# A hybrid decoder layer: TensorE's order in the second part written out as a list, with larger banks and weight pieces

## The chip, the cores and the metric

The kernel runs on one core of a Trainium2 chip. [...] Each engine works through its own instructions in order, and semaphores tie the engines together. The metric is the device time of one launch in microseconds (us).

## The reference

One decoder layer on 256 tokens of width 1024, with two attention branches side by side and an output that must hold in float32. The listing is shortened from the reference's description and its functions.

```python
D_MODEL = 1024; SEQ = 256; MLA_HEADS = MOBA_HEADS = 8      # one sequence, one layer
def one_layer(x, c, positions, p):                          # "a" is MLA, "b" is MoBA
    mod = silu(c) @ W_ada + b_ada;  shift, scale, gate = split(mod)
    h = rms_norm(x, g_pre) * (1 + scale) + shift
    q_lat, kv_lat, k_rope, gate_a, q_b, k_b, v_b, gate_b, merge = split_cols(h @ W_in, IN_SIZES)
    # branch a: queries and keys of 64 + 32 (rope) per head, from latents of rank 256 and 128
    q = rms_norm(q_lat, g_q) @ W_uq;  k_nope, v = split(rms_norm(kv_lat, g_kv) @ W_ukv)
    o_a = causal_dense_attention(concat(q_nope, rope(q_pe)), concat(k_nope, rope(k_rope)), v, 96 ** -0.5)
    # branch b: 64 per head; 256 tokens are one block, so each token sees its own block, causally
    o_b = causal attention of (rope(q_b), rope(k_b), v_b), scale 64 ** -0.5
    y_a = (o_a * silu(gate_a)) @ W_o_a;  y_b = (o_b * silu(gate_b)) @ W_o_b
    y = (sigmoid(merge_a) * y_a + sigmoid(merge_b) * y_b) @ W_out
    return x + gate * rms_norm(y, g_post)
```

## The kernel before

**Accuracy sets the work.** Each float32 operand is split into a rounded part and a remainder, `w1 = round(w)` and `w2 = w - w1`, and each product is three matmuls, `w1·h1 + w1·h2 + w2·h1`. A weight arrives by DMA in a raw tile of 2048 columns, and is split in units of 1024 columns: ACT writes `w1` (L264, `w<-raw`), DVE writes `w2` (L264, `w<-raw,w`). Five units and five raw tiles are alive at a time (`RING`, `RAW`), so a split waits until TensorE has finished the unit five before it. Before, each unit is split in two halves of 512 columns.

**Two parts.** The first part (to 61 us) computes the modulation, the normalised input `h` and the projections of branch b; its order stays as it is. The second part holds all else: 24 units `F` (gates and merge gates; L417 to L419, 24 matmuls of 128x256 each, into the bank "acc"), the latents of branch a (`lat_mm`, L501 to L503), and for each of 16 heads scores, a softmax (DVE and ACT, L660 to L669), three transposes of the probabilities (`p_tr`, L676) and the product with the values (`pv`, L686 and L690); then the output projections `oproj` of b and a, the adaLN gate and the final product `out_mm`.

**Who sets the order.** Before, the second part is written as calls with `fill()` between them, which puts in the next `F`. A scheduler orders each engine, and it mixes the matmuls of neighbouring calls on TensorE. There are four kinds of PSUM bank, "tr", "sc", "acc" and "pv", with two buffers each; whoever asks for a bank waits for the readers of the buffer's last content.

**Names for the steps below.** `lat_stats`, `lat_evac`, `lat_tr` (L509 to L545) read the latents from the two "tr" banks, scale them and transpose them. `moba_tr(w, t)` (L461) transposes half t of branch b's queries (w = 0) or keys (w = 1) into a "tr" bank, which ACT and DVE then read (L464, L472, L473). `uq_nope`, `ukv_nope` (L589 to L591, L610 to L612) make queries and keys of branch a; their banks are read in three steps by DVE, ACT, DVE (L553 to L555 and L559 to L561). `ukv_v` (L619 to L621) makes its values. All four use bank "pv", as `pv` does. `ada_gate` (L712, L714) adds up the adaLN gate on DVE from raw tiles, eight instructions over 1024 columns.

**Narrow shapes.** Scores of b contract over 64 rows (`64*128` in the rows), values write 64 columns (`128*64`); all other matmuls use 96 or 128 rows and 128 columns.

Of the kernel before, what the change touches and what calls it, by code (L numbers as in the profile page):

```python
# [18 lines left out]
P = 128  # L19
D = 1024  # L20
S = 256
# [24 lines left out]
POOL_LOW = []  # L46


def _cut(v, bits):
# [12 lines left out]
def hybrid_layer_kernel(ctx: ExitStack, tc: tile.TileContext, x, cols, pos, cst, gpost, bgate,  # L62
# [7 lines left out]
    mm = nc.tensor.matmul  # L70
# [150 lines left out]
    for key, src, n, parts in stream:  # L221
        if key[0] != "w":
            loads.append((key, src, 0, n))
        if key == ("out", 0, 0):
            order.append(("gate", 0))
            splits += [(("gate", 0), ("gate",), 0, a, a + 512) for a in (0, 512)]
        size = 2 * NL if key[0] == "l" else 1024
        for i, c0 in enumerate(range(0, n, size)):
            m = min(size, n - c0)
            order.append(key + (i,))  # L230
            cut = size // 2
            splits += [(key + (i,), key, c0, a, e) for a, e in ((0, min(cut, m)), (cut, m)) if a < m]
# [16 lines left out]
    def split_one():  # L249
        if not splits:  # L250
            return False
        u, key, c0, a, b = splits[0]
        if key not in raws or got.get(key, 2048) < c0 + b:
            return False
        if a == 0:
            i = order.index(u)
            if i >= RING and order[i - RING] not in finished:
                return False
            w1s[u] = rg.tile([P, 1024], FR, name="w1", bufs=RING)
            w2s[u] = rg.tile([P, 1024], FR, name="w2", bufs=RING)  # L260
        splits.pop(0)
        r = raws[key][:, c0 + a:c0 + b]
        w = key[0] == "w"
        free = lambda eng, f, *a, **k: f(*a, **k)  # L264
        o = ordered if w else free
        if u == ("w", 0, 0) and a == 0:
            o("V", V.tensor_copy, w1s[u][:, a:b], r)
        else:
            o("A", act, w1s[u][:, a:b], r, AF.Copy)
        rel = key != ("gate",) and (not splits or splits[0][1] != key)  # L270
        if w:
            subs.append((u, key, a, b, r, rel))
# [134 lines left out]
    def F():  # L407
        i = fcount[0]
        if i >= 24:
            return  # L410
        fcount[0] += 1
        key = ("f", i // 2, i % 2)
        w1, w2 = weights(key, KT)
        b = bank("acc" if i else "pv")
        o = b[:, :S]
        for k in range(KT):
            mm(o, w1[:, k], h1[:, k], start=(k == 0), stop=False)  # L417
            mm(o, w1[:, k], h2[:, k], start=False, stop=False)  # L418
            mm(o, w2[:, k], h1[:, k], start=False, stop=(k == KT - 1))  # L419
        done_with(key)  # L420
        kind, m = ORDER[i]
        if kind == "g":
            act(tg[m // 8][:, m % 8], o, AF.Tanh, scale=0.5, bias=bmh[:, m:m + 1])
        else:
            th = wk.tile([P, S], FT, name="th", bufs=2)
            act(th, o, AF.Tanh, scale=0.5)
            z = wk.tile([P, S], FT, name="sz", bufs=5)
            V.scalar_tensor_tensor(z, th, 1.0, o, op0=OP.add, op1=OP.mult)
            sz[kind, m] = z


    def rope_nat(b, t, n, fs, dst, eng):
# [199 lines left out]
    def scores(br, h):  # L632
        scale = (96.0 if br == "a" else 64.0) ** -0.5
        if br == "a":
            heads = [h]
            q0, k0 = a0[:, 0], a0[:, 1]
            view = lambda x, i: x[:, i]
        else:
            heads = [h, h + 1] if h % 2 == 0 else []
            q0, k0 = m0[:, 0], m0[:, 1]  # L640
            view = lambda x, i: x[64 * (i % 2):64 * (i % 2) + 64, i // 2]
        for i in heads:
            sct[i] = bank("sc")
        for i in heads:
            mm(sct[i][:, 0:P], view(q0, i), view(k0, i), start=True, stop=True)  # L645
        if br == "b":
            ops = [(mop["q1"], km1), (mop["q2"], km1), (mop["q1"], mop["k2"])]
        else:
            q1, q2 = aop["q"][:, 0], aop["q"][:, 1]
            ops = [(q1, ak1), (q2, ak1), (q1, aop["k2"])]  # L650
        for n, (q, k) in enumerate(ops):
            for i in heads:
                mm(sct[i][:, P:3 * P], view(q, i), view(k, i), start=(n == 0), stop=(n == len(ops) - 1))  # L653
        b = sct.pop(h)
# [23 lines left out]
        act(pT, b[:, :384], AF.Copy)  # L678
        pTt[br, h] = pT

    def pv(br, m):
        v = va if br == "a" else vb
        b = bank("pv")
        for i in range(2):
            h = 2 * m + i
            mm(b[64 * i:64 * i + 64, 0:S], v[0][:, h * 64:h * 64 + 64], pTt[br, h][:, 0:S], start=True, stop=False,  # L686
               skip_group_check=True)
        for i in range(2):
            h = 2 * m + i
            mm(b[64 * i:64 * i + 64, P:S], v[1][:, h * 64:h * 64 + 64], pTt[br, h][:, S:384], start=False, stop=True,  # L690
               skip_group_check=True)
# [4 lines left out]
        u = wk.tile([P, S], FT, name="u", bufs=2)  # L696
        V.tensor_tensor(u, b[:, :S], sz[br, m], op=OP.mult)
        act(u1[br][:, m], u, AF.Copy)
        V.tensor_tensor(u2[br][:, m], u, u1[br][:, m], op=OP.subtract)


    gt = {}
# [54 lines left out]
        G.tensor_tensor(y2[:, m], yy, y1[:, m], op=OP.subtract)  # L757


    fillers = [F] * 24 + [lambda m=m: oproj("b", m) for m in range(8)]  # L760

    def fill(n=1):
        for _ in range(n):
            if fillers:
                fillers.pop(0)()
# [7 lines left out]
    lat_evac()  # L773
    moba_tr(0, 0)
    moba_tr(0, 1)
    lat_tr()
    fill()
    moba_tr(1, 0)
    moba_tr(1, 1)
    fill()  # L780
    uq_pe()
    scores("b", 0)
    fill()
    uq_nope(0)
    scores("b", 1)
    uq_nope(1)
    p_tr("b", 0)
    scores("b", 2)
    p_tr("b", 1)
    pv("b", 0)  # L790
    fill()
    ukv_nope(0)
    scores("b", 3)
    p_tr("b", 2)
    fill()
    ukv_nope(1)
    ukv_v(0)
    qpe_tr()
    ukv_v(1)
    heads = [("b", h) for h in range(4, 8)] + [("a", h) for h in range(8)]  # L800
    prev = ("b", 3)
    done = []
    for n, hd in enumerate(heads):
        scores(*hd)
        fill()
        if done:
            pv(*done.pop(0))
        p_tr(*prev)
        if prev[1] % 2 == 1:
            done.append((prev[0], prev[1] // 2))  # L810
        prev = hd
        if n % 4:
            fill()
        if n == 5:
            ada_gate_load()
        if 6 <= n < 10:
            ada_gate(n - 6)
    if done:
        pv(*done.pop(0))
    fill(2)  # L820
    p_tr(*prev)
    fill(1)
    pv("a", 3)
    fill(8)
# [54 lines left out]
    for t, c0, n, tag in ((0, 0, 512, "tr"), (1, 0, 256, "tr"), (1, 256, 256, "pv")):  # L879
        b = bank(tag)  # L880
        for kg in range(2):
            out_mm(1, kg, t, b, c0, n)
        out_part(t, 512 + c0, n, b)


_C_INS = ["cols", "pos", "cst", "gpost", "bgate", "wada", "wadag", "win1", "winl", "win2", "wuq", "wukv", "wo", "wout"]
# [60 lines left out]
```

## Time and profile before

| | us |
|---|---|
| median of three runs (lowest, highest) | 235.46 (233.86, 235.47) |
| the profiled execution | 236.85 |
| its span, first to last instruction | 235.1 |
| busy in it: TensorE, DVE, ACT, POOL | 223.1, 169.0, 134.7, 50.8 |

A profiled execution is one launch seen instruction by instruction; its own time is 1.39 us above the median of the three. Busy times of engines overlap. Matmuls are pipelined: a row's duration is longer than the step to the next start, so stretches of TensorE are measured from start to start.

### The profile page before, as it was taken

Reading aid. Unit: us, or ns where it says so; the run is one execution under the profiler, and the core shown is the slowest. Engines: PE = TensorE matmul, PEld = TensorE weight load, DVE = VectorE, ACT = ScalarE, POOL = GpSimd, SP = SyncE. Lnnn points to the kernel's source line nnn. Section 1 sums busy time; section 2 is a strip of 40 time slices with the busy share of each in tenths; the row PEclk is TensorE's granted clock in tenths of the full one; section 3 lists DMA queues with packets and bytes.
Section 4 is the critical chain, followed back from the end, with each engine's and each line's share of the span. In section 5 each row is a group of like instructions: output and inputs, shape, how many; then the busy total and the mean of one; then the engine's idle time right before and its main releaser. Section 6 shows DMA issues by size and latency. Waiting matters only on the chain.

```text
span 235.1 us, 4288 instructions
## 1 busy us (share of the span) xinstructions
PE 223.1 (95%) x1558; PEld 190.6 (81%) x1558; DVE 169.0 (72%) x415; ACT 134.7 (57%) x320; POOL 50.8 (22%) x82
## 2 busy tenths in 40 slices
PE   8679999999899999999999999999999999999990
PEld 8255666666699999999979988989999899988890
DVE  1462455444799767989979998999987566899543
ACT  4262444555866478649765996547477433664320
POOL 1138888500045101500000000000400000463000
PEclk9877999999999999999999999999999999999997
DMA  6999788898985534250550515789789720000022
GB/s 199 362 404 403 253 295 277 298 303 314 337 331 180 198 163 178 92 180 0 184 178 1 181 25 206 287 287 326 265 315 419 282 96 3 1 0 3 0 89 89
DMA packets 10679, 47.05 MB, mean 200 GB/s; under 512 B 1441, under 2 KB 2081, under 8 KB 7586
## 3 DMA queue, kind: packets, MB, share of 16 engines
q1 hardware_dynamic: 10658, 46.78, 55.5%
q8 instruction: 12, 0.20, 0.3%
q14 instruction: 9, 0.07, 0.1%
HBM read 45.73 MB, written 1.05 MB: 199 GB/s over the span
## 4 chain that ended last, share of the span: by engine, by line
PE 87%; DMA 3%; DVE 2%; issue 2%; ACT 1%; SPq 1%; POOLq 0%; POOL 0%; DVEq 0%; ACTq 0%
PE acc L417 9%; PE acc L419 9%; PE acc L418 9%; PE sc L81 6%; PE acc L81 5%; PE pv L81 5%; PE tr L81 5%; PE pv L686 3%; DMA raw<-in_wada_dram 3%; PE acc L745 3%; PE tr L676 2%; PE acc L747 2%; PE acc L746 2%; PE sc L653 2%; PE sc L645 2%
## 5 line engine op out<-in xcount | busy, mean ns | idle before, releaser
L264 ACT ACTIVATE w<-raw 128x512 fp32r<-128x512 f32 (+1 forms) x93 | 52.4, 617 | 34.3 <-PE acc L418 11.0
L264 DVE TENSOR_TENSOR w<-raw,w 128x512 fp32r<-128x512 f32 (+1 forms) x93 | 63.8, 727 | 6.2 <-ACT w L264 5.3
L417 PE MATMUL acc<-h,w 128*128 128x256 f32 x184 | 53.0, 288 | 0.1
L419 PE MATMUL acc<-h,w 128*128 128x256 f32 x184 | 52.8, 287 | 0.0
L418 PE MATMUL acc<-h,w 128*128 128x256 f32 x184 | 52.3, 284 | 0.0
L417 PEld LDWEIGHTS acc<-h,w 128*128 128x128 f32 x184 | 34.7, 188 | 1.2 <-issue 0.7
L419 PEld LDWEIGHTS acc<-h,w 128*128 128x128 f32 x184 | 34.7, 188 | 0.6
L418 PEld LDWEIGHTS acc<-h,w 128*128 128x128 f32 x184 | 34.7, 188 | 0.3
L81 DVE TENSOR_TENSOR w<-raw,w 128x512 fp32r<-128x512 f32 x24 | 16.8, 729 | 14.6 <-ACT w L81 14.2
L81 PE MATMUL acc<-w,h 128*128 128x512 f32 x48 | 16.1, 420 | 1.3 <-ACT h L81 1.3
L717 POOL TENSOR_TENSOR gacc<-gacc,bgt 1x1024 f32<-1x1024 f32 x1 | 2.6, 2570 | 67.7 <-PE acc L418 67.7
L81 PE MATMUL pv<-w,h 128*128 128x512 f32 x48 | 16.0, 418 | 1.0 <-ACT w L81 1.0
L81 PE MATMUL sc<-w,h 128*128 128x512 f32 x48 | 16.4, 426 | 0.3 <-ACT w L81 0.3
L757 POOL TENSOR_TENSOR y<-yy,y 128x256 fp32r<-128x256 f32 x8 | 8.5, 1074 | 37.3 <-ACT y L756 37.3
L665 ACT ACTIVATE p<-p,mx 128x128 f32<-128x128 f32 (+1 forms) x32 | 14.2, 445 | 0.1
L81 ACT ACTIVATE w<-raw 128x512 fp32r<-128x512 f32 x23 | 13.5, 618 | 0.0
L81 PEld LDWEIGHTS acc<-w,h 128*128 128x128 f32 x48 | 8.8, 194 | 5.5 <-ACT h L81 3.9
L81 PEld LDWEIGHTS pv<-w,h 128*128 128x128 f32 x48 | 8.6, 193 | 4.5 <-ACT w L81 3.2
L81 PEld LDWEIGHTS sc<-w,h 128*128 128x128 f32 x48 | 7.9, 189 | 4.6 <-issue 3.1
L443 POOL TENSOR_TENSOR rr<-rr,m 128x512 f32<-128x512 f32 x4 | 5.6, 1420 | 25.6 <-DVE m L442 25.6
L678 ACT ACTIVATE pT<-tr 128x384 f32<-128x384 f32 x16 | 7.7, 486 | 5.7 <-PE tr L676 5.6
L81 ACT ACTIVATE rws<-tr 128x256 f32<-128x256 f32 x7 | 2.7, 384 | 14.4 <-PE tr L81 14.4
(250 smaller groups left out, 529.8 us busy)
## 6 DMA issues: line engine op xcount, KB each, us to landing
raw<-in_win_dram SPq DMA_DIRECT2D x12, 1024.0 KB, 4.8
raw<-in_wada_dram SPq DMA_DIRECT2D x16, 512.0 KB, 6.1
raw<-in_win_dram SPq DMA_DIRECT2D x8, 512.0 KB, 6.6
raw<-in_wadag_dram SPq DMA_DIRECT2D x4, 1024.0 KB, 4.9
raw<-in_wo_dram SPq DMA_DIRECT2D x4, 1024.0 KB, 4.8
raw<-in_wout_dram SPq DMA_DIRECT2D x4, 1024.0 KB, 9.4
raw<-in_win_dram SPq DMA_DIRECT2D x8, 256.0 KB, 6.8
raw<-in_winl_dram SPq DMA_DIRECT2D x2, 832.0 KB, 6.3
```

What stands on the lines that cost most here:

```text
L81: r = f(*a, **k)
L264: free = lambda eng, f, *a, **k: f(*a, **k)
L417: mm(o, w1[:, k], h1[:, k], start=(k == 0), stop=False)
L418: mm(o, w1[:, k], h2[:, k], start=False, stop=False)
L419: mm(o, w2[:, k], h1[:, k], start=False, stop=(k == KT - 1))
L443: eng.tensor_tensor(dst, dst, m2, op=OP.add)
L645: mm(sct[i][:, 0:P], view(q0, i), view(k0, i), start=True, stop=True)
L665: act(p[:, a:e], p[:, a:e], AF.Exp, scale=scale, bias=mx[:, t:t + 1], accum_out=sm[:, t:t + 1])
L678: act(pT, b[:, :384], AF.Copy)
L686: mm(b[64 * i:64 * i + 64, 0:S], v[0][:, h * 64:h * 64 + 64], pTt[br, h][:, 0:S], start=True, stop=False, skip_group_check=True)
L745: mm(o, w1[:, k, c0:c0 + P], u1[br][:, k], start=(k == 0), stop=False)
L757: G.tensor_tensor(y2[:, m], yy, y1[:, m], op=OP.subtract)
```

## The change

The second part's TensorE order is fixed by a list of tokens, `plan`, inside a block that takes TensorE away from the scheduler; the other engines are still ordered by it. Tokens: `F` a unit; `q00` to `q11` are `moba_tr(w, t)`; `l` the three steps on the latents; `up` and `un0`, `un1` the queries of a, `un2`, `un3` its keys, `uv` both values, `pe` the transpose of rotated queries; `sb0` is `scores("b", 0)` and so on (now two heads of b at once, their softmaxes behind both); `tb0` is `p_tr`, `vb0` is `pv` of four heads into one bank; `g`, `G0` to `G3` the gate's sum; `B` an output projection of b. Weights of the second part are split in pieces of a whole unit (1024 columns; 832 for the latents). The gate's raw tiles are loaded after those of `oproj`, and its sum stands near the end. The buffers change with it: `u` is one of 512 columns, `sz` three of 512, `th` shares with `hf`.

```diff
-            splits += [(("gate", 0), ("gate",), 0, a, a + 512) for a in (0, 512)]
+            splits.append((("gate", 0), ("gate",), 0, 0, 1024))
...
-            cut = size // 2
-            splits += [(key + (i,), key, c0, a, e) for a, e in ((0, min(cut, m)), (cut, m)) if a < m]
-        if key[0] == "f" and key[1] >= 8:
-            loads.append((("g", key[1] - 8), wadag[key[1] - 8], 0, 2048))
+            cut = 512 if key[0] == "w" else m
+            splits += [(key + (i,), key, c0, a, min(a + cut, m)) for a in range(0, m, cut)]
+        if key[0] in ("ob", "oa"):
+            i = 2 * (key[0] == "oa") + key[1]
+            loads.append((("g", i), wadag[i], 0, 2048))
...
-            heads = [h, h + 1] if h % 2 == 0 else []
+            heads = [h, h + 1]
...
+        for i in heads:
+            softmax(br, i, scale)
...
-    def pv(br, m):
+    def pv(br, g):
...
-        for i in range(2):
-            h = 2 * m + i
-            mm(b[64 * i:64 * i + 64, 0:S], v[0][:, h * 64:h * 64 + 64], pTt[br, h][:, 0:S], start=True, stop=False,
+        for n in range(4):
+            h, c0, q = 4 * g + n, S * (n // 2), 64 * (n % 2)
+            mm(b[q:q + 64, c0:c0 + S], v[0][:, h * 64:h * 64 + 64], pTt[br, h][:, 0:S], start=(n < 2), stop=False,
...
-    lat_mm()
+    plan = """F q00 q01 F l F q10 q11 F up sb0 F un0 un1 F tb0 tb1 pe sb2 F un2 un3 uv F tb2 tb3 sb4 F vb0 F tb4 tb5 sb6
+        F F sa0 tb6 tb7 F sa1 vb1 F ta0 sa2 F ta1 sa3 F ta2 sa4 F ta3 sa5 F va0 F ta4 sa6 F ta5 sa7 F F g ta6 F F G0 ta7
+        B G1 B G2 va1 B G3 B B B B B"""
...
+    ops = dict(F=F, l=lat_all, up=uq_pe, un0=lambda: uq_nope(0), un1=lambda: uq_nope(1), un2=lambda: ukv_nope(0),
+               un3=lambda: ukv_nope(1), uv=ukv_values, pe=qpe_tr, g=ada_gate_load, B=lambda: oproj("b", next(obs)))
...
+    in_order = tc.manual_schedule(engines={mybir.EngineType.PE})
+    in_order.__enter__()
+    with tc.issue_after(last_ins["T"]):
+        lat_mm()
     for w in range(2):
         for t in range(2):
             moba_rope(w, t)
-    fill()
-    lat_stats()
...
+    for tok in plan.split():
+        run(tok)
```

The instruction order of both programs shows what moves. Lines of the changed program have other numbers (its L416 to L418, L460, L609 to L611, L618 to L620, L690 and L694 are L417 to L419, L461, L610 to L612, L619 to L621, L686 and L690 of before).

TensorE around the transposes of b's keys, before: the first four (one half of the tokens) stand among the matmuls of a unit `F`, whose rows are `acc<-h,w`.

```order
L417 MATMUL acc<-h_162,w_969 128x256
L418 MATMUL acc<-h_163,w_969 128x256
L419 MATMUL acc<-h_162,w_970 128x256
L461 MATMUL tr<-cstt,rr 128x128 x4
L417 MATMUL acc<-h_162,w_1045 128x256
L418 MATMUL acc<-h_163,w_1045 128x256
L419 MATMUL acc<-h_162,w_1046 128x256
```

The other four, before, stand some forty rows later, after two matmuls of `uq_nope` and others.

```order
L591 MATMUL pv<-ql_694,w_771 128x256
L418 MATMUL acc<-h_163,w_1045 128x256
L419 MATMUL acc<-h_162,w_1046 128x256
L417 MATMUL acc<-h_162,w_1045 128x256
L461 MATMUL tr<-cstt,rr 128x128 x4
L645 MATMUL sc<-m_680 128x128 x2
```

The same place now: both halves stand in one run of eight (`q10 q11`), between the end of one `F` and the start of the next.

```order
L416 MATMUL acc<-h_162,w_722 128x256
L417 MATMUL acc<-h_163,w_722 128x256
L418 MATMUL acc<-h_162,w_723 128x256
L460 MATMUL tr<-cstt,rr 128x128 x8
L416 MATMUL acc<-h_162,w_738 128x256
L417 MATMUL acc<-h_163,w_738 128x256
L418 MATMUL acc<-h_162,w_739 128x256
```

What moved: the two halves were apart, with two other products between them; now the second half follows the first at once.

TensorE around branch a's second key product (`ukv_nope(1)` is the rows above before's fence; here `kl` are the latents), before: first the key product's end, then an `F` and other work.

```order
L610 MATMUL pv<-kl_696,w_919 128x256
L611 MATMUL pv<-kl_697,w_919 128x256
L612 MATMUL pv<-kl_696,w_920 128x256
L417 MATMUL acc<-h_162,w_1358 128x256
L418 MATMUL acc<-h_163,w_1358 128x256
```

Before, the first value product (L619 to L621) stands some fifteen rows further on, between transposes of probabilities.

```order
L418 MATMUL acc<-h_163,w_1412 128x256
L676 MATMUL tr<-cstt,p 128x128 x2
L619 MATMUL pv<-w_919,kl_696 128x512
L620 MATMUL pv<-w_920,kl_696 128x512
L621 MATMUL pv<-w_919,kl_697 128x512
L676 MATMUL tr<-cstt,p 128x128
L419 MATMUL acc<-h_162,w_1413 128x256
```

The same place now: keys and values in one run, all into bank "pv".

```order
L610 MATMUL pv<-kl_687,w_854 128x256
L611 MATMUL pv<-kl_686,w_855 128x256
L609 MATMUL pv<-kl_686,w_854 128x256
L610 MATMUL pv<-kl_687,w_854 128x256
L611 MATMUL pv<-kl_686,w_855 128x256
L618 MATMUL pv<-w_854,kl_686 128x512
L619 MATMUL pv<-w_855,kl_686 128x512
L620 MATMUL pv<-w_854,kl_687 128x512
```

DVE's rows over the same place now: its reading of the key banks (L558 `a<-pv`, L560 `raw<-pv,ak`) stands among a weight split (L274), a gate product `sz`, rotated queries (`a<-tr`, `raw<-tr`) and two softmaxes (`sm`, `p`).

```order
L669 RECIPROCAL sm<-sm 128x2
L672 TENSOR_SCALAR p<-p,sm 128x128
L672 TENSOR_SCALAR p<-p,sm 128x256
L560 TENSOR_TENSOR raw<-pv,ak_683 64x2x256
L558 COPY a_682<-pv 64x2x128
L560 TENSOR_TENSOR raw<-pv,ak_683 64x2x256
L672 TENSOR_SCALAR p<-p,sm 128x128
L672 TENSOR_SCALAR p<-p,sm 128x256
L558 COPY a_682<-pv 64x2x128
L554 TENSOR_TENSOR raw<-tr,raw 32x2x128
L560 TENSOR_TENSOR raw<-pv,ak_683 64x2x256 x2
L274 TENSOR_TENSOR w_1290<-raw,w_1289 128x1024
```

What moved: the values' banks are those that the rows L560 read last; before, two other stretches of TensorE's work lay between.

TensorE at values of b, before (L686 and L690, 64 columns each), among transposes and an `F`.

```order
L418 MATMUL acc<-h_163,w_1514 128x256
L686 MATMUL pv<-pT,vbt 64x256 x2
L690 MATMUL pv<-pT,vbt 64x128 x2
L686 MATMUL pv<-pT,vbt 64x256
L676 MATMUL tr<-cstt,p 128x128 x3
L419 MATMUL acc<-h_162,w_1515 128x256
L417 MATMUL acc<-h_162,w_1514 128x256
L686 MATMUL pv<-pT,vbt 64x256
L690 MATMUL pv<-pT,vbt 64x128 x2
L676 MATMUL tr<-cstt,p 128x128 x3
L418 MATMUL acc<-h_163,w_1514 128x256
```

The same step now, four heads in one run of sixteen matmuls.

```order
L417 MATMUL acc<-h_163,w_1275 128x256
L418 MATMUL acc<-h_162,w_1276 128x256
L690 MATMUL pv<-pT,vbt 64x256 x4
L694 MATMUL pv<-pT,vbt 64x128 x4
L416 MATMUL acc<-h_162,w_1279 128x256
```

What moved: pieces of two, four and six narrow matmuls became one run of sixteen.

## Rows read from the trace of the kernel before

**Rows 1.** The page: busy time, and the chain that ended last.

```profile
PE 223.1 (95%) x1558; PEld 190.6 (81%) x1558; DVE 169.0 (72%) x415; ACT 134.7 (57%) x320; POOL 50.8 (22%) x82
...
PE 87%; DMA 3%; DVE 2%; issue 2%; ACT 1%; SPq 1%; POOLq 0%; POOL 0%; DVEq 0%; ACTq 0%
```

**Rows 2.** TensorE's waits over the span: total, times and longest, the first of seven.

```profile
PE acc L81 <- ACT h L81: 1.3, 1, 1.3
```

**Rows 3.** Windows: span, busy time (instructions) of each engine, clock, DMA share, GB/s.

```profile
100.00:120.00 20.00, 19.86 (x156) 18.17 (x155) 17.88 (x64) 14.52 (x42) 0.00 (x0) 1.00 0.44 140
```

**Rows 4.** Timeline of TensorE: a scores stretch of four matmuls and one of ten.

```profile
96.32 0.49 PE L645 MATMUL sc<-m 64*128 64x128 f32 x4
96.74 0.39 PE L418 MATMUL acc<-h,w 128*128 128x256 f32 x1
...
106.13 0.59 PE L645 MATMUL sc<-m 64*128 64x128 f32 x3
...
107.33 0.39 PE L417 MATMUL acc<-h,w 128*128 128x256 f32 x1
```

**Rows 5.** Timeline of TensorE: value stretches of two, six and ten matmuls.

```profile
117.11 0.65 PE L686 MATMUL pv<-pT,vbt 128*64 128x256 f32 x2
117.68 0.39 PE L610 MATMUL pv<-kl,w 128*128 128x256 f32 x1
117.91 0.28 PE L611 MATMUL pv<-kl,w 128*128 128x256 f32 x1
118.03 0.28 PE L612 MATMUL pv<-kl,w 128*128 128x256 f32 x1
...
138.43 0.65 PE L686 MATMUL pv<-pT,vbt 128*64 128x256 f32 x4
...
139.66 0.55 PE L676 MATMUL tr<-cstt,p 128*128 128x128 f32 x3
...
140.38 0.43 PE L686 MATMUL pv<-pT,vbt 128*64 128x256 f32 x1
...
141.17 0.44 PE L676 MATMUL tr<-cstt,p 128*128 128x128 f32 x2
```

**Rows 6.** Lines by form from 60 us: weight splits, the gate's sum.

```profile
L264 DVE TENSOR_TENSOR w<-raw,w 128x512 fp32r<-128x512 f32 x85 | 59.7, 740 | 6.2 <-ACT w L264 5.3 <-PE acc L419 0.5
...
L714 DVE SCALAR_TENSOR_TENSOR gacc<-raw,sc,gacc 128x1024 f32<-128x1024 f32 x7 | 8.9, 1277 | 0.0
```

**Rows 7.** Timeline of TensorE and ACT at the latents.

```profile
77.47 0.28 PE L417 MATMUL acc<-h,w 128*128 128x256 f32 x1
...
81.60 0.38 ACT L519 ACTIVATE kvlat<-tr,rsl 128x128 f32<-128x128 f32 x1
```

**Rows 8.** Timeline of ACT and DVE around the keys' first transpose.

```profile
90.73 1.15 ACT L264 ACTIVATE w<-raw 128x512 fp32r<-128x512 f32 x2 [0.89 <-PE acc L418]
...
92.72 0.36 ACT L544 ACTIVATE ak<-tr 32x256 fp32r<-32x256 f32 x1
...
93.45 2.00 DVE L547 CAST ak<-ak 32x1792 fp32r<-32x1792 f32 x1
95.47 0.69 DVE L473 TENSOR_TENSOR km<-tr,km 128x512 fp32r<-128x512 f32 x1
```

**Rows 9.** Timeline of DVE and TensorE between branch a's key and value products.

```profile
118.69 0.42 DVE L559 COPY a<-pv 64x256 f32<-64x256 f32 x1 [0.83 <-PE pv L612]
...
120.36 0.68 DVE L561 TENSOR_TENSOR raw<-pv,ak 64x512 fp32r<-64x512 f32 x1
...
124.71 0.69 DVE L561 TENSOR_TENSOR raw<-pv,ak 64x512 fp32r<-64x512 f32 x1
...
128.50 0.48 PE L619 MATMUL pv<-w,kl 128*128 128x512 f32 x1
```

**Rows 10.** Windows of TensorE, first part: busy time, clock, DMA share, GB/s.

```profile
10.00:12.00 2.00, 1.67 (x14) 0.50 1.03 415
...
18.00:20.00 2.00, 2.00 (x18) 0.50 1.02 400
```

More of the change, by code (lines that the diff above doesn't have):

```diff
@@ L45 @@
 LAST = "P0v P1v P2v V P0q P0k P1q P2q P1k P2k"
-POOL_LOW = []
 def _cut(v, bits):
@@ L273, in split_one @@
             return True
-        eng = "G" if (order.index(u), a // 512) in POOL_LOW else "V"
-        free(eng, dict(V=V, G=G)[eng].tensor_tensor, w2s[u][:, a:b], r, w1s[u][:, a:b], op=OP.subtract)
+        V.tensor_tensor(w2s[u][:, a:b], r, w1s[u][:, a:b], op=OP.subtract)
         if rel:
@@ L424, in F @@
         else:
-            th = wk.tile([P, S], FT, name="th", bufs=2)
+            th = wk.tile([P, S], FT, name="th", tag="hf", bufs=2)
             act(th, o, AF.Tanh, scale=0.5)
-            z = wk.tile([P, S], FT, name="sz", bufs=5)
-            V.scalar_tensor_tensor(z, th, 1.0, o, op0=OP.add, op1=OP.mult)
-            sz[kind, m] = z
+            if m % 2 == 0:
+                sz[kind, m // 2] = wk.tile([P, 2, S], FT, name="sz", bufs=3)
+            V.scalar_tensor_tensor(sz[kind, m // 2][:, m % 2], th, 1.0, o, op0=OP.add, op1=OP.mult)
     def rope_nat(b, t, n, fs, dst, eng):
@@ L653, in scores, with softmax @@
                 mm(sct[i][:, P:3 * P], view(q, i), view(k, i), start=(n == 0), stop=(n == len(ops) - 1))
+        for i in heads:
+            softmax(br, i, scale)
+    def softmax(br, h, scale):
         b = sct.pop(h)
@@ L679, in p_tr @@
         pTt[br, h] = pT
-    def pv(br, m):
+    def pv(br, g):
         v = va if br == "a" else vb
         b = bank("pv")
-        for i in range(2):
-            h = 2 * m + i
-            mm(b[64 * i:64 * i + 64, 0:S], v[0][:, h * 64:h * 64 + 64], pTt[br, h][:, 0:S], start=True, stop=False,
+        for n in range(4):
+            h, c0, q = 4 * g + n, S * (n // 2), 64 * (n % 2)
+            mm(b[q:q + 64, c0:c0 + S], v[0][:, h * 64:h * 64 + 64], pTt[br, h][:, 0:S], start=(n < 2), stop=False,
                skip_group_check=True)
-        for i in range(2):
-            h = 2 * m + i
-            mm(b[64 * i:64 * i + 64, P:S], v[1][:, h * 64:h * 64 + 64], pTt[br, h][:, S:384], start=False, stop=True,
+        for n in range(4):
+            h, c0, q = 4 * g + n, S * (n // 2), 64 * (n % 2)
+            mm(b[q:q + 64, c0 + P:c0 + S], v[1][:, h * 64:h * 64 + 64], pTt[br, h][:, S:384], start=False, stop=True,
                skip_group_check=True)
@@ L695, in pv @@
             u2[br] = sb.tile([P, 4, S], FR, name="u2" + br, tag=t2)
[L696 to L699, printed above, removed]
+        u = wk.tile([P, 2, S], FT, name="u", bufs=1)
+        d1, d2 = (x[br][:, 2 * g:2 * g + 2] for x in (u1, u2))
+        V.tensor_tensor(u, b.rearrange("p (k n) -> p k n", k=2), sz[br, g], op=OP.mult)
+        act(d1, u, AF.Copy)
+        V.tensor_tensor(d2, u, d1, op=OP.subtract)
     gt = {}
@@ L757, in oproj, with ukv_values, lat_all, run @@
         G.tensor_tensor(y2[:, m], yy, y1[:, m], op=OP.subtract)
[L760 to L765, printed above, removed]
-    lat_mm()
+    plan = """F q00 q01 F l F q10 q11 F up sb0 F un0 un1 F tb0 tb1 pe sb2 F un2 un3 uv F tb2 tb3 sb4 F vb0 F tb4 tb5 sb6
+        F F sa0 tb6 tb7 F sa1 vb1 F ta0 sa2 F ta1 sa3 F ta2 sa4 F ta3 sa5 F va0 F ta4 sa6 F ta5 sa7 F F g ta6 F F G0 ta7
+        B G1 B G2 va1 B G3 B B B B B"""
+    def ukv_values():
+        ukv_v(0)
+        ukv_v(1)
+    def lat_all():
+        lat_stats()
+        lat_evac()
+        lat_tr()
+    obs = iter(range(8))
+    ops = dict(F=F, l=lat_all, up=uq_pe, un0=lambda: uq_nope(0), un1=lambda: uq_nope(1), un2=lambda: ukv_nope(0),
+               un3=lambda: ukv_nope(1), uv=ukv_values, pe=qpe_tr, g=ada_gate_load, B=lambda: oproj("b", next(obs)))
+    def run(tok):
+        if tok in ops:
+            ops[tok]()
+        elif tok[0] == "G":
+            ada_gate(int(tok[1]))
+        elif tok[0] == "q":
+            moba_tr(int(tok[1]), int(tok[2]))
+        else:
+            dict(s=scores, t=p_tr, v=pv)[tok[0]](tok[1], int(tok[2]))
+    in_order = tc.manual_schedule(engines={mybir.EngineType.PE})
+    in_order.__enter__()
+    with tc.issue_after(last_ins["T"]):
+        lat_mm()
     for w in range(2):
@@ L770, in hybrid_layer_kernel @@
             moba_rope(w, t)
-    fill()
-    lat_stats()
[L773 to L824, printed above, removed]
+    for tok in plan.split():
+        run(tok)
+    assert fcount[0] == 24 and next(obs, None) is None and not pt
     y1 = sb.tile([P, 8, S], FR, name="y1", tag="hy1")
@@ L883, in hybrid_layer_kernel @@
         out_part(t, 512 + c0, n, b)
+    in_order.__exit__(None, None, None)
 _C_INS = ["cols", "pos", "cst", "gpost", "bgate", "wada", "wadag", "win1", "winl", "win2", "wuq", "wukv", "wo", "wout"]
```

## The prediction

> **What bounds the kernel now.** I read the page first: TensorE is busy for 223.1 of 235.1 us, and 87% of the chain that ended last is its own [rows 1]. The list of waits then shows that nothing stops it for long: seven waits, the longest 1.3 us, all on lines of the first part [rows 2]. In the second part it is full, while DVE is not far behind: in the window shown DVE has work for 17.88 of 20 us [rows 3]. So before, the second part lasts as long as TensorE's matmuls take, and a change pays in two ways only: by TensorE time that goes, and against it by waits that did not exist. DVE leaves little room to catch up if it comes to be waited for.
>
> **What goes: switches to narrow shapes.** A 256-column matmul starts 0.12 us after the one ahead (117.91 to 118.03), but around a stretch of 64 rows or 64 columns the steps are longer: the first full matmul after it takes 0.23 us instead (117.68 to 117.91) [rows 5]. With about 0.1 us ahead and behind, a value stretch of two costs 0.57 + 0.11 + 0.09 = 0.77 us; one of six 0.79 + 0.2 = 0.96; the one of ten 1.23 + 0.1 = 1.37 [rows 5]. Over the whole trace there are six, six and one of these (the rows show one of each), and a mixed one whose value part is about 0.96: 4.6 + 5.8 + 1.4 + 1.0 = 12.7 us. After, four stretches of sixteen hold the same matmuls: the first pair 0.77, three more pairs of 256 columns at 0.21 and four of 128 columns at 0.095 (the differences between those stretches) make 1.77 us each, 7.1 in all. Scores of b: ten matmuls in one stretch took 1.20 + 0.2 = 1.4 us, four alone 0.42 + 0.2 = 0.62 [rows 4]; before there are nine stretches, 7.2 us by the same sums, after four of ten, 5.6. Together **-7.3 us** of TensorE time. This holds in any order that keeps the stretches whole, and I give it 6.5 to 7.5. The other matmuls stay the same in number and shape.
>
> **What is added: the list's own waits.** Before, when a matmul was not ready, the order had another one there. A fixed list cannot step round, so I walked it with durations of the rows, stop by stop.
>
> *Queries of b (`q00 q01` after the first `F`).* Both take the "tr" banks that hold the latents, free only when ACT has scaled them. Before, that ended at 81.60 + 0.38 = 81.98, 4.5 us after the first `F` ended at 77.47 [rows 7], and TensorE spent the time on two more units. Now the transposes follow the first `F` at once. The scaling may come somewhat earlier, since fewer splits lie ahead on ACT and DVE: 2 to 4.5 us, and I take 3.0, between the two.
>
> *Keys of b (`q10 q11`).* The other "tr" bank still holds the shared rope key, whose last reader now stands late on DVE, so q11 must take q10's own bank, and wait until DVE has read it. That read stands behind a chain that starts when the unit ahead ends: on ACT a split, a tanh and the latents' reads, from 90.73 to 92.72 + 0.36 before, about 2.2 us with one split instead of two; then DVE's copy of 2.00 us, then the read at 0.69 [rows 8]. That is 4.9 us, less 0.5 for q10 itself: **4.4 us**, from 3.5 (splits done early) to 5.
>
> *Rotated queries (`pe`).* They need the bank of the first `tb`, whose ACT read stands behind a split (1.0) and the next tanh. Split, tanh and the read itself, the last two put at 0.3 and 0.5 beside the 0.36 of the narrower read in [rows 8], are 1.8 us, less 0.7 for the two `tb`: 1.1 us, from 0 to 1.5. The second halves of the products `un2 un3` wait 0.4 us for DVE's read of `un1`.
>
> *Keys and values of a (`un2 un3 uv`).* All four products use the two "pv" banks, so the values wait until DVE has read both key banks. Before, a key product's bank was free 7 us after its matmuls: its reads ran from 118.69 to 124.71 + 0.69, among two softmaxes, and the value product came at 128.50 [rows 9]. After, DVE's rows ahead of that point are one split, one gate product, four copies like 118.69 (0.35 to the next start), three subtractions like 120.36 (0.65), three reads of rotated queries (0.42, of the same 256 columns) and two softmax tails (384 columns and a reciprocal, estimated from the same row at 0.6 each): 1.2 + 0.35 + 1.4 + 1.95 + 1.3 + 1.2 = 7.4 us, and they start when ACT's split is there, 1.0 us after the unit ahead has ended. Key products take 12 x 0.12 = 1.4 us of these 8.4 and their own wait 0.4: **6.5 us**, from 5 to 7.3.
>
> *Late stretch.* The gate's sum, eight DVE instructions of which seven took 8.9 us [rows 6], moves to where DVE must also read b's output projections, eight of twelve matmuls, 1.4 us each on TensorE. DVE there gets about as much work as TensorE; two stops follow on my walk, at the seventh `B` and at the gate's second half. From 0 to 4 us; I take 2.3. The transfers for the sum move behind those of the output projections on SP's queue; I cost that at nothing, since eight projections of a hide them, and if they come late the same stop grows.
>
> *The clock.* In the first part, after short idle times, 10 to 12 us and 18 to 20 us ran at a granted clock of 0.50, that is 1.2 instead of 2.4 GHz, and TensorE was busy for 1.67 and 2.00 us of them [rows 10]; work there takes twice its time, so such a stretch gives away about 0.8 to 1.0 us. In the second part the clock was 1.00 [rows 3]. Three of the stops above are longer than any idle time in the trace of before. I take two falls of some 1 us, 2.0 in all, from 0 to 4.5. The Trainium skill speaks against such stops too: its page "TensorE: Matmul & The Clock Gate" (section "HAM oscillation — how this bites in real kernels") says that a kernel whose TensorE waits between short bursts is throttled anew after each wait, and by that rule each of the three long stops would be followed by a half-rate stretch; the rows of the first part agree, while the rows of the second show full speed, having no such stop.
>
> *Pieces of 1024 columns.* Two splits of 512 (DVE 0.74 each [rows 6]) become one, perhaps 0.1 us shorter on DVE and on ACT. TensorE waits for neither, since units are split ahead of need; only where a stop has its cause in DVE does this help, by less than 0.2 us. Softmaxes in pairs and the smaller buffers of `u` and `sz` move DVE work by one head; in the middle part, from the eighth unit to the last scores, the walk found no stop, as each read has at least one unit (2.9 us) of cover.
>
> **Sum.** 3.0 + 4.4 + 1.1 + 0.4 + 6.5 + 2.3 = 17.7 us of stops, 2.0 for the clock, less 7.3: +12.4. Against the profiled execution that is 236.85 + 12.4 = 249.3; the profiled execution lies 1.4 above the median of three, so I predict **248** us. With the low ends of the terms (2 + 3.5 + 0 + 0 + 5 + 0, no clock) it is 238.7, with the high ends (4.5 + 5 + 1.5 + 0.5 + 7.3 + 4 + 4.5) 255.5.
>
> **Rivals.**
> *The list keeps TensorE full.* If DVE and ACT read each bank before the list gets there, only the 7.3 us are left: 228. For it: the waits of before are few, and whoever wrote a list could have placed each token behind its cover. Against it: `q10 q11` and `un3 uv` stand without a single matmul between writer and next user of a bank, and the rows of before show 5 and 7 us from write to free bank there.
> *The stops are about half.* DVE idles while TensorE waits, so what is late catches up, and a stop paid early pays for later ones; with 9 us of stops and a full clock the sum is +1.7, 237. For it: DVE had slack around the latents. Against it: the stops' chains are counted from the end of a unit that itself waited, so slack ahead of them does not shorten them.
> *More stops than the walk found.* DVE at nine tenths [rows 3] sets the pace in the middle part as well, because each of its delays now reaches TensorE; two units' time more, 5.7 us: 254.
> *The clock falls after every long stop.* Each of the three is followed by stretches at 0.50 as long as the 2 us rows of the first part, twice over, 1.5 us lost apiece: 4.5 instead of 2.0, and 250.5. For it: the first part's rows, whose idle times were shorter. Against it: the stop is followed by dense matmuls, and 100 to 120 us shows that these hold 1.00. This is the rule of the page named above.
>
> **How the numbers follow.** Forecast (243 to 250): 0.45; the clock after every stop (249 to 253): 0.12; list keeps TensorE full (225 to 232): 0.14; half the stops (233 to 242): 0.17; more stops (252 to 258): 0.12. What lies below 235 and above 255 adds up to some 0.2, so the range is 235 to 255. One per cent, 2.4 us, is about what a measurement of this kernel can tell from no change: faster than that holds the first rival, 0.14; within it lies a third of the half-stops case and a little of the rest, 0.07; slower, with the forecast, the clock, the more stops and most of the half, is 0.79.
>
> **What would show it.** In the profile after, the list of waits should show TensorE waiting in the second part: at the transposes of b's keys for DVE's `km`, about 4 us; at the value product for DVE's reads of the keys, about 6; at b's first queries for ACT's latents, about 3. Value stretches of sixteen should last near 1.8 us. The granted clock should fall to 0.50 after at least one long stop. The prediction is wrong if these waits are under 1 us each, if DVE's copies overlap the stops in another order, or if the late stretch ends as before.

## The result, and the profile after

The changed kernel takes 256.97 us (254.52 to 260.55, four runs) against 235.47: 1.087 times the time before, 95% interval 1.080 to 1.094. It is slower, as forecast, but by 21.5 us, where 12.4 were forecast; 255, the upper end of the range, was passed by 2 us. The profiled execution shown here is the slowest of the four, with the lowest clock (0.927; the others 0.953 to 0.967), so its clock part is probably larger than the median's. In the rows PE is TensorE and PEld its weight loads, DVE is VectorE, ACT ScalarE, POOL GpSimd, and SP SyncE, which issues the DMA transfers; TensorE writes banks of PSUM, and in both traces only DVE and ACT read them.

The page of the changed kernel: TensorE does the same work in a longer span [rows 1]. The shares of the chain add up to 15% of the span here, against 96% before: the page could not follow it back through the second part, so it does not tell what bounds the kernel now. The waits do.

```profile
PE 224.0 (87%) x1558; PEld 195.2 (76%) x1558; DVE 164.4 (64%) x360; ACT 130.2 (50%) x269; POOL 53.2 (21%) x82
...
PE 7%; DVE 3%; issue 3%; POOL 1%; ACT 1%; POOLq 0%; DVEq 0%; ACTq 0%
```

The list of TensorE's waits (line, what it waited for: total, times, longest), the rows of the second part. Before there was none of these [rows 2].

```profile
PE pv L618 <- DVE raw L560: 7.7, 1, 7.7
PE tr L460 <- DVE km L472: 4.7, 1, 4.7
PE tr L460 <- POOL rsl L512: 3.4, 1, 3.4
...
PE acc L750 <- DVE tg L756: 1.5, 1, 1.5
PE pv L609 <- DVE raw L554: 1.5, 1, 1.5
PE pv L737 <- DVE yy L759: 1.4, 1, 1.4
PE pv L737 <- DVE gpt L739: 1.2, 1, 1.2
...
PE tr L599 <- ACT pT L681: 1.1, 1, 1.1
```

Eight waits, 22.5 us. Seven stand at a place that the prediction's walk had named; the wait for `yy`, at the gate's first half, it had not. At b's queries the list names POOL's `rsl`, but that had ended at 80.23 us; the transposes started at 81.10, when ACT's scaling of the latents had ended at 81.00, which is the wait that was walked. Measured from start to start less the step that a matmul has anyway, the same eight are 24.0 us.

ACT and DVE around the keys' first transpose, and TensorE's second (the answer to [rows 8]):

```profile
90.06 1.06 ACT L264 ACTIVATE w<-raw 128x1024 fp32r<-128x1024 f32 x1 [0.91 <-PE acc L417]
...
92.04 0.35 ACT L543 ACTIVATE ak<-tr 32x256 fp32r<-32x256 f32 x1
...
92.43 2.01 DVE L546 CAST ak<-ak 32x1792 fp32r<-32x1792 f32 x1
94.47 0.69 DVE L472 TENSOR_TENSOR km<-tr,km 128x512 fp32r<-128x512 f32 x1
...
89.98 0.60 PE L460 MATMUL tr<-cstt,rr 128*128 128x128 f32 x4
95.31 1.09 PE L460 MATMUL tr<-cstt,rr 128*128 128x128 f32 x4 [4.73 <-DVE km L472]
```

The chain is the one that was walked, link by link: the unit ahead ends, ACT splits, reads a rope key, DVE copies for 2.01 us and then reads the first half's bank, and only then does TensorE go on, after 4.73 us of standing. At the values (the answer to [rows 9]) DVE's reads lie among a split, rotated queries and softmax tails, and the first value matmul starts when the third subtraction is done:

```profile
121.39 1.22 DVE L274 TENSOR_TENSOR w<-raw,w 128x1024 fp32r<-128x1024 f32 x1
122.63 0.42 DVE L428 SCALAR_TENSOR_TENSOR sz<-th,acc 128x256 f32<-128x256 f32 x1
122.97 0.74 DVE L558 COPY a<-pv 64x256 f32<-64x256 f32 x2
...
125.36 0.68 DVE L560 TENSOR_TENSOR raw<-pv,ak 64x512 fp32r<-64x512 f32 x1
...
128.58 1.30 DVE L560 TENSOR_TENSOR raw<-pv,ak 64x512 fp32r<-64x512 f32 x2
...
129.42 0.77 PE L618 MATMUL pv<-w,kl 128*128 128x512 f32 x1 [7.74 <-DVE raw L560]
```

Windows of TensorE (span, busy time and instructions, granted clock, DMA share, GB/s) in and after the stops, to be held against [rows 3, 10]:

```profile
82.00:84.00 2.00, 2.00 (x11) 0.50 1.01 426
...
92.00:94.00 2.00, 0.00 (x0) 1.00 0.35 143
94.00:96.00 2.00, 0.69 (x4) 0.57 0.00 0
96.00:98.00 2.00, 2.00 (x11) 0.50 0.22 82
98.00:100.00 2.00, 2.00 (x11) 0.50 0.57 180
...
126.00:128.00 2.00, 0.00 (x0) 0.50 0.00 0
...
130.00:132.00 2.00, 2.00 (x6) 0.50 0.00 0
132.00:134.00 2.00, 2.00 (x10) 0.50 0.00 0
...
228.00:230.00 2.00, 2.00 (x5) 0.50 0.00 0
```

After each of four stops TensorE works at half its clock, 1.2 instead of 2.4 GHz, for about three to six microseconds, though it has matmuls without a gap there (eleven in 2 us instead of eighteen). Summed over these matmuls, start to start, against their steps at full clock, that is 1.2 + 2.4 + 2.7 + 1.5 = 7.8 us. The fourth is the second of the gate's two; behind the stops of 1.1 and 1.5 us at `pe`, at `un2` and at the seventh `B` no fall is seen. The Trainium skill's page "TensorE: Matmul & The Clock Gate" (section "HAM oscillation — how this bites in real kernels") describes a kernel that waits for DMA between bursts and is throttled anew after each wait. This trace agrees for the three long stops, of 3.6, 4.9 and 7.9 us, where the waits are for ACT and DVE.

A value run and a scores run of the changed kernel, answering to [rows 4, 5]:

```profile
140.94 1.08 PE L690 MATMUL pv<-pT,vbt 128*64 128x256 f32 x8
141.85 0.61 PE L694 MATMUL pv<-pT,vbt 128*64 128x128 f32 x8
142.39 0.39 PE L416 MATMUL acc<-h,w 128*128 128x256 f32 x1
...
146.08 0.49 PE L644 MATMUL sc<-m 64*128 64x128 f32 x4
146.33 0.60 PE L652 MATMUL sc<-km,qm 64*128 64x256 f32 x6
146.86 0.39 PE L416 MATMUL acc<-h,w 128*128 128x256 f32 x1
```

Sixteen value matmuls take 1.45 us, 1.65 with the longer steps around them; ten scores 0.78 and 0.97, not 1.4 as the ten of before. All narrow stretches together, summed from start to start with the longer steps around them as in the prediction, fell from 19.9 to 10.5 us: 9.4 saved.

**The account of the span**, 235.1 to 258.4 us: narrow runs -9.4, stops +24.0, half clock +7.8, sum +22.4 of 23.3 us; the remaining 0.9 is not assigned.

### The profile page after: what moved, and what is told of

Read it like the earlier page. It is cut to its first block, busy times and chain, and to the rows that moved or that the text cites. A ratio compares the mean times of both kernels' runs of the same rounds, so it can differ in the third digit from the quotient of the medians.

```text
span 258.4 us, 4173 instructions
## 1 busy us (share of the span) xinstructions
PE 224.0 (87%) x1558; PEld 195.2 (76%) x1558; DVE 164.4 (64%) x360; ACT 130.2 (50%) x269; POOL 53.2 (21%) x82
## 5 line engine op out<-in xcount | busy, mean ns | idle before, releaser
L274 DVE TENSOR_TENSOR w<-raw,w 128x1024 fp32r<-128x1024 f32 (+2 forms) x47 | 59.9, 1282 | 25.8 <-ACT w L264 25.7
L264 ACT ACTIVATE w<-raw 128x1024 fp32r<-128x1024 f32 (+2 forms) x47 | 48.3, 1033 | 44.6 <-PE acc L417 21.4
L416 PE MATMUL acc<-h,w 128*128 128x256 f32 x184 | 55.1, 299 | 0.0
L417 PE MATMUL acc<-h,w 128*128 128x256 f32 x184 | 53.7, 292 | 0.0
L418 PE MATMUL acc<-h,w 128*128 128x256 f32 x184 | 53.6, 291 | 0.0
L416 PEld LDWEIGHTS acc<-h,w 128*128 128x128 f32 x184 | 36.9, 201 | 1.2 <-issue 0.5
L417 PEld LDWEIGHTS acc<-h,w 128*128 128x128 f32 x184 | 36.8, 200 | 0.1
L418 PEld LDWEIGHTS acc<-h,w 128*128 128x128 f32 x184 | 36.8, 200 | 0.0
L722 POOL TENSOR_TENSOR gacc<-gacc,bgt 1x1024 f32<-1x1024 f32 x1 | 3.2, 3238 | 103.5 <-DVE gacc L719 103.5
L80 PE MATMUL pv<-w,h 128*128 128x512 f32 x48 | 15.8, 417 | 1.0 <-ACT w L80 1.0
L663 DVE CUSTOM_DVE_ANT_0 p<-sc,cstt 128x128 f32<-128x128 f32 (+1 forms) x32 | 10.1, 354 | 3.1 <-PE sc L652 2.9
L762 POOL TENSOR_TENSOR y<-yy,y 128x256 fp32r<-128x256 f32 x8 | 10.2, 1285 | 7.4 <-ACT y L761 4.1
L460 PE MATMUL tr<-cstt,rr 128*128 128x128 f32 x16 | 3.6, 387 | 8.1 <-DVE km L472 4.7
```

The costliest lines, as they stand in the source:

```text
L80: r = f(*a, **k)
L274: V.tensor_tensor(w2s[u][:, a:b], r, w1s[u][:, a:b], op=OP.subtract)
```

## The experiments

Medians, and the ratio to the kernel before that ran on the same chip beside each (its medians there 235.3, in the last four runs 236.3, and 235.5 for the changed kernel's 256.97).

| run | what | us | ratio (95%) |
|---|---|---|---|
| e1_sched | no list | 233.17 | 0.994 (0.989 to 0.998) |
| e2_uv | keys and values of a apart | 257.71 | 1.094 (1.086 to 1.103) |
| e3_three | three repairs | 250.96 | 1.057 (1.047 to 1.068) |
| e4_busy | three stops filled | 255.80 | 1.078 (1.066 to 1.090) |
| e6_whole | no list, narrow runs whole | 228.05 | 0.966 (0.959 to 0.973) |
| e7_half | no list, pieces of 512 | 234.20 | 0.998 (0.993 to 1.003) |
| e8_gate | no list, gate sum early | 234.11 | 0.996 (0.991 to 1.001) |
| e9_banks | both of these | 233.67 | 0.994 (0.989 to 0.998) |
| e10_keys | one repair, keys of b | 254.17 | 1.071 (1.062 to 1.080) |
| e11_gate | one repair, the gate | 253.76 | 1.076 (1.070 to 1.082) |
| e12_mid | list in the middle only | 239.26 | 1.016 (1.008 to 1.023) |
| e13_busy | seven of eight stops filled | 252.09 | 1.069 (1.064 to 1.075) |

### The list alone: e1_sched

```diff
-    in_order = tc.manual_schedule(engines={mybir.EngineType.PE})
-    in_order.__enter__()
...
-    in_order.__exit__(None, None, None)
```

> The changed kernel with TensorE given back to the scheduler; the list is only the order in which the code is written, and wide value banks, paired scores, pieces of 1024 columns and the late gate sum all stay. Theory (the fixed order's stops, 22 us with the clock falls behind them, are the whole loss): the stops go, 228 to 236 us, and no wait of TensorE over 2 us in the second part. Rival (pieces, banks or the late gate sum make DVE and ACT late): 248 us or more, with waits still there.

233.17 us: with everything else of the change kept, the loss is gone, and the only wait in the second part is one of 0.9 us at an output projection:

```profile
PE acc L750 <- DVE tg L756: 0.9, 1, 0.9
```

The fixed order is the whole loss. It is also only a little faster than before, since the scheduler broke up the narrow runs again (17.4 us of them).

### Pieces and the gate sum: e7_half, e8_gate, e9_banks

```diff
-            cut = 512 if key[0] == "w" else m
+            cut = size // 2
```

> TensorE left to the scheduler, as in the run without the list, but weights split in two halves of 512 columns as before. Theory (pieces of 1024 only save a little of DVE and ACT, which TensorE does not wait for): within 1% of the run without the list, 232 to 235 us. Rival (pieces are the gain of that run over the kernel before): 235 us or more.

```diff
-        if key[0] in ("ob", "oa"):
+        if key[0] == "f" and key[1] >= 8:
...
-... F ta0 sa2 F ta1 sa3 F ta2 sa4 F ta3 sa5 F va0 ... F F g ta6 F F G0 ta7 B G1 B G2 va1 B G3 B B B B B
+... F ta0 g sa2 F ta1 G0 sa3 F ta2 G1 sa4 F ta3 G2 sa5 F va0 G3 ... F F ta6 F F ta7 B B va1 B B B B B B
```

> TensorE left to the scheduler, as in the run without the list, but the gate's transfers and its sum early, as before. Theory (where the sum stands costs under 1 us as long as TensorE's order is free; the run without the list waits 1.1 us for DVE at an output projection): 231.5 to 234 us, that wait gone. Rival (the late place relieves DVE in the softmax stretch): 235 us or more, with waits there.

The ninth run joins both edits.

> TensorE left to the scheduler, with halves of 512 columns and the early gate sum as before: of the change only paired scores, values of four heads in one bank, the smaller buffers and the code order of the list are left. Theory (what the run without the list gains comes from the narrow runs): 232 to 235 us. Rival (it comes from pieces and gate): 235.5 us or more.

234.20, 234.11 and 233.67 against 233.17: all four overlap in their intervals. Neither the pieces nor the place of the gate's sum can be told from nothing while TensorE's order is free; the prediction had costed the pieces so. In e8_gate's trace the wait of 0.9 us is gone, and the time is no lower. What the late gate sum costs under the list was not tried alone.

### The narrow runs kept whole, without the list: e6_whole

The sixteen value matmuls and the matmuls of a pair's scores are put in an ordered region of their own, with the operand that is ready last at the head.

```diff
-        for n in range(4):
+        with tc.manual_schedule(engines={mybir.EngineType.PE}):
+            for n in (3, 2, 1, 0):
...
-            ops = [(mop["q1"], km1), (mop["q2"], km1), (mop["q1"], mop["k2"])]
+            ops = [(mop["q1"], mop["k2"]), (mop["q1"], km1), (mop["q2"], km1)]
```

> TensorE left to the scheduler as in the first of these runs, with pieces, banks and late gate sum of the change; only the narrow runs are kept whole: the sixteen value matmuls of four heads, and the scores of a pair, are each an ordered run that begins with the operand that is ready last. In the run without the list the narrow stretches were still 17.4 us of TensorE (19.9 before, 10.5 with the list). Theory (the change's gain is whole narrow runs, which need an order only inside themselves): 11 to 13 us of narrow stretches, no long wait, 4 to 6 us below the run without the list, so 227 to 230 us. Rival (a run that waits for its last operand comes late and TensorE or DVE waits elsewhere): 233 us or more.

228.05 us, 3.4% below the kernel before: narrow stretches 13.1 us, and TensorE waits nowhere in the second part; all rows of its list of waits belong to the first part:

```profile
PE acc L326 <- DMA cstt<-in_cst_dram: 1.9, 1, 1.9
PE acc L80 <- ACT h L80: 1.2, 1, 1.2
PE pv L80 <- ACT w L80: 1.0, 1, 1.0
PE pv L313 <- POOL mhalf L121: 1.0, 1, 1.0
PE tr L82 <- POOL rs L319: 0.7, 1, 0.7
```

19.9 - 13.1 = 6.8 us of TensorE time became 7.3 us of the median. The order holds only inside a run, and the scheduler still put other matmuls between: three of the four value runs and one of the four scores runs are whole in the trace, hence 13.1 and not 10.5. This is the first rival's 228, reached without the list: the saving was real, and the list gave it away.

### Repairing the list: e2_uv, e3_three, e10_keys, e11_gate

```diff
-F q00 q01 F l F q10 q11 F up sb0 F un0 un1 F tb0 tb1 pe sb2 F un2 un3 uv F tb2
+F q00 q01 F l F q10 q11 F up sb0 F un0 un1 F tb0 tb1 un2 un3 pe sb2 F F uv tb2
```

> The changed kernel with one repair of the list: the keys of branch a one unit earlier in part, the values one unit later, so that two units F stand between the last key product and the values. Theory: the stop of 7.7 us at the values shrinks to under 2, and the clock fall behind it (some 3 us) goes: 245 to 249 us. Rival (DVE is simply behind, and what is not waited for here is waited for at the next token): the wait moves on, 254 us or more.

```diff
+F F q00 q01 F l F q10 up F q11 un0 un1 sb0 F un2 un3 tb0 tb1 pe sb2 F F uv tb2
```

> The changed kernel with three repairs of the list: two units ahead of the queries' transposes, a unit between the two halves of the keys' transposes, two units between the last key product and the values. Theory: of 3.4 + 4.7 + 7.7 us of stops some 3 stay, the three clock falls go: 232 to 239 us. Rival (DVE is behind everywhere): 246 us or more.

```diff
-q10 q11 F up sb0 F
+q10 F q11 up sb0 F
```

> The changed kernel with one repair of the list: a unit F between the two halves of the keys' transposes. Theory (this stop is the wait for the first half's own bank, 4.7 us, and a clock fall behind it): under 2.5 us of it stay and the fall goes, 251 to 254 us. Rival (the wait moves to the next token, as it did when the keys and values of branch a were moved): 256 us or more.

```diff
     for m in range(8):
         oproj("a", m)
-    ada_gate_out()
...
     for kg in range(2):
         for t in range(2):
             out_mm(0, kg, t, banks[t], 0, 512)
...
+        if not kg:
+            ada_gate_out()
```

> The changed kernel with the gate's four matmuls moved behind the first sixth of the final product, so that DVE has read the banks of the last output projections before. Theory: the two stops there, 2.6 us, and the clock fall behind them, some 1.5 us, go: 252.5 to 254.5 us. Rival (DVE is late with the split of the final weights, and TensorE waits for those instead): 256 us or more.

Where the products that follow do not need DVE, a repair pays by the traces: the gate's 2.6 us of stops and the clock fall behind them go (253.76); at the keys of b 4.7 us become 1.9, but a half-rate stretch, from 96.1 to 99.5 us, still follows (254.17, just above what the theory gave). The medians alone are near the limit of what can be told: the interval of e11_gate (1.070 to 1.082) touches the changed kernel's (1.080 to 1.094). And in e10_keys the gate's stops of 1.4 and 1.2 us are still there, with no fall behind them until the last matmul:

```profile
220.00:250.00 30.00, 24.19 (x127) 0.99 0.06 21
```

So that fall is not in every execution, and how much of e11_gate's 3.2 us it was is open. Where they do need it, the wait moved, as the rival said, and I was wrong: with the values two units further on (e2_uv) the stop of 7.7 is gone, that at `un2` has grown and one at `tb2` is new,

```profile
PE pv L609 <- DVE raw L554: 4.4, 1, 4.4
...
PE tr L679 <- DVE raw L554: 2.7, 1, 2.7
```

and TensorE's stops, from start to start, fell from 24.0 to 20.7 us without a gain, with five falls of the clock instead of four; with three repairs (e3_three, 250.96 us, in the rival's range) those at b's queries and at the values are all but gone and one of 6.5 us stands at `un2`. DVE in that run, while TensorE stood from 101.62 to 108.16 for the reads L554:

```profile
99.83 1.21 DVE L274 TENSOR_TENSOR w<-raw,w 128x1024 fp32r<-128x1024 f32 x1
...
102.17 0.17 DVE L669 RECIPROCAL sm<-sm 128x2 f32<-128x2 f32 x1 [0.98 <-ACT p L668]
...
104.26 1.23 DVE L274 TENSOR_TENSOR w<-raw,w 128x1024 fp32r<-128x1024 f32 x1
105.93 0.42 DVE L554 TENSOR_TENSOR raw<-pv,raw 64x256 fp32r<-64x256 f32 x1 [0.44 <-ACT raw L553]
...
107.60 0.95 DVE L554 TENSOR_TENSOR raw<-pv,raw 64x256 fp32r<-64x256 f32 x2
```

The read that TensorE needs stands behind two splits and the ends of two softmaxes that it doesn't need yet, for which DVE itself waits on ACT for 0.98 us. Each new list gets a new DVE order from the scheduler, and in this one the read that the list comes to next is not put first. Whether a list exists whose stops are all covered was not found out.

### The list where no stop was seen: e12_mid

```diff
-    for tok in plan.split():
-        run(tok)
+    toks = plan.split()
+    cut = toks.index("uv") + 1
+    for tok in toks[:cut]:
+        run(tok)
+    with tc.manual_schedule(engines={mybir.EngineType.PE}):
+        for tok in toks[cut:]:
+            run(tok)
```

The block around the whole list is taken out.

> The changed kernel with the list in force only from the unit behind the values of branch a to the last output projection of b; TensorE before and behind it is left to the scheduler. Theory (the middle of the list costs nothing, its stops all lie in its first stretch and its end): the stops of the first stretch, 18.4 us, and the clock falls behind them go, 231 to 236 us, with the wait of 1.5 us at an output projection left. Rival (a fixed order also costs in the middle, where the walk found no stop): 240 us or more.

239.26 us, above what the theory gave and just below the rival's 240. TensorE ran from 140 to 180 us without a pause at full clock, so the middle of the list does cost nothing:

```profile
140.00:180.00 40.00, 40.00 (x346) 1.00 0.55 198
```

But stops of 3.9 us at `un2` and 1.9 us at the values, with some 3 us lost to half clock behind them, stand just ahead of the region. The likely cause is that the scheduler no longer had the later units to put in there; no run shows it.

### Stop or clock: e4_busy, e13_busy

Matmuls whose result nobody reads are put inside the stops (`D`, 24 of 128x256; `d`, 10); the output is that of the kernel.

```diff
+    def idle_work():
+        b = bank("acc")
+        for k in range(24):
+            mm(b[:, :S], h1[:, k % 8, 0:P], h1[:, k % 8], start=(k == 0), stop=(k == 23))
...
+F D q00 q01 F l F q10 D q11 F up sb0 F un0 un1 F tb0 tb1 pe sb2 F un2 un3 D D uv F tb2
```

> The changed kernel with work added inside the three long stops: 24 matmuls of 128x256 whose result is not read (2.9 us) after the first F and between the two halves of the keys' transposes, and 48 before the values. DVE's order is that of the changed kernel. Theory (stops cost their length and then a clock fall): the stops end when they did, the granted clock stays at 1.00 there, and the time falls by the clock's part alone, 4 to 8 us: 249 to 253 us. Rival (the clock costs nothing of its own, it only marks idle time): 256 to 258 us. If the added matmuls did lengthen the stops: above 258.

255.80 us, in neither theory's span (249 to 253, 256 to 258): the added 11.4 us of matmuls made no stop end later, and no half-rate stretch follows the first two stops any more, but others came behind what was still open (the last 2.0 us at the values, then the gate's stops: 1.4 us lost near 130, 2.9 us near 225). That left the cause undecided, so matmuls were put at all eight.

```diff
+F D q00 q01 F l F q10 D d q11 F up sb0 F un0 un1 F tb0 tb1 d pe sb2 F d un2 un3 D D d uv F tb2
...
+B G3 B B B d B B          # and 11 matmuls ahead of each half in ada_gate_out
```

> The changed kernel with matmuls whose result is not read inside every stop of the second part: 24, 34 and 58 of 128x256 in the three long ones, 10 or 11 in each of the five short ones. The earlier run of this kind filled three and still had clock falls behind the others. Theory (the clock falls where TensorE stood still, and only there): no half-rate stretch in the second part, and the time falls by all of the clock's part, to 248 to 251 us. Rival (the falls have another cause): stretches at 0.50 are still there, 253 us or more.

252.09 us (251.80 to 252.46). Windows of TensorE in this run, the first two with all the long stops:

```profile
61.00:100.00 39.00, 37.81 (x275) 1.00 0.54 198
100.00:140.00 40.00, 39.02 (x328) 1.00 0.19 69
```

The changed kernel's own:

```profile
61.00:100.00 39.00, 30.55 (x180) 0.88 0.56 201
100.00:140.00 40.00, 29.64 (x221) 0.86 0.15 54
```

No matmul of the second part is at half clock, and the time is 1 us above what I expected of it. One stop was not filled: the matmuls at the seventh `B` ask for an "acc" bank themselves, so they waited as the projection had,

```profile
PE acc L786 <- DVE tg L759: 1.5, 1, 1.5
```

and the projection came behind them, 3.10 us after the matmul ahead (200.63 to 203.73) instead of 1.80 (208.06 to 209.86): 1.3 us added. The chains on ACT and DVE are as long as ever at the three long stops, so what fell is the clock's part: 256.97 - 252.09 = 4.9 us of the median, some 6 with the 1.3 taken off. The two were not run side by side; each held against the kernel before that ran beside it, 21.5 and 15.8 us, they differ by 5.7. In the profiled executions the time from one and the same matmul near the start of the second part (at 61.31 and at 60.41 us) to the end is 197.1 and 190.3 us: 6.8 less, 8.1 with the 1.3, beside the 7.8 summed above. That the clock's falls in the second part come from TensorE's stops is shown for this kernel; that every stop brings one is not so.

## Why the prediction was wrong

**The direction and the places were right.** Seven of the eight waits stand where the walk put them; b's queries 3.6 us (3.0 predicted, 2 to 4.5), keys 4.9 (4.4, 3.5 to 5), rotated queries 1.3 (1.1, 0 to 1.5).

**Mis-sized: the clock, the step "I take two falls of some 1 us, 2.0 in all".** There were four, of 1.2 to 2.7 us, 7.8 in the profiled execution and 4.9 to 6 in the median. The rows that I priced them by were windows of 2 us in the first part, and I counted a fall as one such window; TensorE worked at half clock for about 3 to 6 us after a stop. This step alone, at its measured size, takes the forecast to 251 to 254 us. The rival of a fall after every stop had the mechanism, and its 4.5 us was nearest, if still too small.

**Mis-sized: three stops, 6.3 us together, the largest miss.** The values 7.9 us (6.5; the upper bound was 7.3), because DVE, held by the softmax reads of a pair and by copies of queries, came to the split ahead of these reads only at 121.39, when the key products were all but done (the last started at 121.41), so that nothing of the chain lay beside them; the chain itself took 7.9 us, to 129.27, where I had summed 7.4. The key products 1.7 (0.4), in one stop ahead of the first of them: a whole pair of softmax reads lay ahead of DVE's read of `un1`. The late stretch 4.7 (2.3, 0 to 4): three stops, not two; I had seen the seventh `B` and the gate's second half, but not that the gate's first half takes a bank of the last output projections. Together 17.7 became 24.0.

**Mis-sized the other way: the saving.** 9.4 instead of 7.3 us. I took ten scores at the 1.4 us that they had in the order of before, where heads of a pair did not alternate; alternating, pairs start within 8 ns of each other and the ten take 0.97. Four times that is 1.7 us; the value runs, 1.65 instead of 1.77, are the rest. The errors of the three terms add up to -2.1 + 6.3 + 5.8 = 10.0 of the 11.3 us by which the profiled execution was missed (249.3 forecast, 260.55); 0.9 of the rest is the unassigned part of the span.

**The rivals.** "The list keeps TensorE full" named the right time, 228, for the wrong kernel: the narrow runs whole, without the list, give it. "The stops are about half" fell: they came to 24.0 us, not 9, and the keys' chain began at the end of the unit ahead, as the walk had it. "DVE sets the pace in the middle" fell too: from 140 to 200 us TensorE ran at 20.00 of 20 us. "Pieces of 1024 columns" at nothing is borne out by e7_half, for a free order; under the list it was not tried alone.

## What to carry to other kernels

A hand-written order for one engine is only as good as the distance, at each step, between a write to a bank and the next claim on it; read that distance off the trace of before, on the reading engines' own queues, and fix the order only where all inputs are at hand. Here that meant inside a narrow run, headed by its latest operand: 7.3 us gained instead of 21.5 lost. And price TensorE's stops with the half clock behind them, which here was a fifth to a third of their sum again (4.9 in the median, 7.8 in the profile, of 24.0 us).

## What had not been expected of the hardware

Filling a stop with useless matmuls made the kernel faster: seven filled stops, 4.9 us less in the median, and runs that agree within 0.7 us where the unfilled kernel's spread over 6. In the changed kernel the clock went to 0.50 while TensorE stood and stayed there for up to 5.8 us of gapless matmuls (129.4 to 135.2). And narrow matmuls whose halves of rows or columns alternate start 4 to 8 ns apart in pairs, and a pair of value matmuls takes one step, 0.1 us for 128 columns and 0.2 for 256.
